# Output product of both token chunks in the front part, with one split of its weights, and the first layer norm statistics beside it

## The chip, the cores and the metric

The kernel runs on one core of a Trainium2 chip. A core has a matrix engine (TensorE, PE in the profile), a vector engine (VectorE, DVE), an activation engine (ScalarE, ACT), a general engine (GpSimd, POOL), a sync engine that issues most transfers (SyncE, SP), and 16 DMA engines. Each engine runs its own list of instructions in order; semaphores order them against each other. The metric is the device time of one execution, in microseconds (us).

## The reference, cut to what matters

One layer of a decoder trunk over 1024 prompt tokens and 8 x 8 sample tokens. Two token mixers (sparse attention and gated linear attention) run on the same input; what follows them is what the change touches:

```python
    branch_a = attn @ w_attn_o
    branch_b = o_b @ w_gla_o
    merged = jax.nn.sigmoid(z['gate_a']) * branch_a + jax.nn.sigmoid(z['gate_b']) * branch_b
    return merged @ w_out, k_a, v_a, k_i, s_new.astype(x.dtype)

def residual_block(x, mix_out, ln1_g, ln1_b, w_ff1, w_ff2, ln2_g, ln2_b):
    h = layer_norm(DN_ALPHA * x + mix_out, ln1_g, ln1_b)
    ff = jnp.square(jax.nn.relu(h @ w_ff1)) @ w_ff2
    return layer_norm(DN_ALPHA * h + ff, ln2_g, ln2_b)
```

Widths: 1024 model features, 4096 FF features. `layer_norm` takes the mean and the mean square over the features of each token. DN_ALPHA is 2 ** 0.25.

## The kernel before, in words

**Tiles.** Features lie on the 128 partitions, tokens along the free axis. The 1088 tokens are three chunks, counted from zero here as in the code: chunk 0 (tokens 0 to 383), chunk 1 (384 to 767), chunk 2 (768 to 1087, the rest of the prompt and the samples). A 1024 x 1024 weight is eight columns `f` of eight 128 x 128 blocks `k`.

**Split products.** Every product of full precision is three matmuls of a reduced-precision type (`mm3`): a weight and an input are split into a high half (an ACT copy that rounds) and a low half (a DVE or POOL subtraction of the high half), and TensorE adds high x high, high x low and low x high. A 128-column of `w_out` for one chunk is thus 8 x 3 = 24 matmuls of 128 x 384. Each weight costs a load (SP), an ACT copy and a subtraction.

**Front and back.** `front` holds the projections, both mixers for the prompt, and at its end the jobs that mix the branches (`mix_job`) and the output product of chunk 0 (`project_job`, matmuls into `pwo`). `back` opens other pools over the same memory. Its `project` runs the output product of chunk 1 (`outputs`), loading and splitting `w_out` a second time, then `feed` runs the feed-forward network in blocks of four or eight FF1 columns and all eight FF2 columns, for chunks 0 and 1 together, with the samples' attention (`at_scores`, `at_values`) in between, and then for chunk 2.

**Layer norm** (`ln`). The residual sum `z` is 8 tiles of 128 x 384 (`zx` for chunk 0, `z` for chunk 1); POOL adds them to one tile (`ls`, or the third part of `zx`) as they come. One matmul of ones gives the mean (`plm`); DVE subtracts it, ACT squares (`lq`), DVE and POOL add up the squares (`ls2`, `ls3`); one set of matmuls gives the mean square (`plv`); ACT takes the root and DVE the reciprocal (`lr`); TensorE spreads it (`plr`); DVE scales each `z`, ACT adds the bias and rounds to the high half of `h`, DVE makes the low half.

**FF stage.** `ff1_first` runs the first four FF1 columns side by side, over `k` as the tiles of `h` appear. `ff1_out` squares the positive part: ACT, DVE, ACT (high half of `a`), DVE or POOL (low half). `ff2_pair` runs the first two FF2 columns side by side, over the first three FF1 outputs and then the fourth; `ff2_out` adds to `acc`, the first time with two DVE operations that also add ALPHA times the two halves of `h`.

**What sets the order.** The code of each job is a generator that says what it needs next. `Order.run` steps the first generator whose needs are due, by a model of each engine's clock (`Clock`), and the instructions stand on each engine in the order in which they are so emitted. `Clock.take` models which buffer of a pool comes free first. All engine calls go through one helper, so they all have the same line in the profile (L260); tiles tell them apart. In the names of tiles, `w`, `wh`, `wl` are the halves of split weights, `wr` raw weights, `mg` the split merged branches, `sum` the merged branch of chunk 1 before its split.

In the front, weights of a job are loaded and split ahead of it into pages (`page`, 34 pages in two groups), which are free again after the job.

## Time and profile before

| | us |
|---|---|
| median of 3 runs | 2049.19 |
| lowest and highest run | 2048.11 and 2050.15 |
| the profiled execution | 2050.56 |
| its span, first to last instruction | 2048.9 |

The span is one execution on the chip. The profile gives for each engine its busy time and, for an idle stretch, the instruction that ended it (the releaser). A stretch of the span can be asked for with the busy time of each engine and the clock that TensorE was granted, as a share of full speed; a timeline lists one engine's instructions, equal neighbours merged, with the time at which a group starts and how long it lasts. Matmuls overlap: one of 128 x 384 is listed with 0.33 us and starts 0.17 us after the one before.

The front ends at about 1066 us, with the last product of chunk 0. The product of chunk 1 follows until 1109, then FF1 (to 1132) and FF2 (to 1153) of chunk 0, then FF1 and FF2 of chunk 1.

### The profile page before, as it was taken

The page shows a single profiled execution, that of the slowest core. Times are in us where ns is not written, and L with a number is a line of the kernel's source. Part 1 is how long each engine was busy: PE and PEld are TensorE (multiplying, and loading weights), DVE is VectorE, ACT ScalarE, POOL GpSimd, SP SyncE. Part 2 cuts the span into 40 slices and gives each one's busy share as a digit, 9 for nine tenths or more (in the row PEclk, how much of TensorE's full clock was granted, in tenths as well). Part 3 has the DMA queues.
Part 4 walks back from the last instruction along what each step waited for, and adds up shares of the span by engine and source line. Part 5 has one row for each costly group of instructions (what it writes and reads, how often), then busy time and mean ns, then how long its engine had stood idle before and what let it go on. Part 6 is the DMA issues. An engine that isn't in the chain of part 4 may idle for free.

```text
span 2048.9 us, 34577 instructions
## 1 busy us (share of the span) xinstructions
PE 2017.5 (98%) x12439; PEld 1949.7 (95%) x12439; DVE 1250.1 (61%) x2624; ACT 1115.4 (54%) x2217; POOL 787.4 (38%) x585
## 2 busy tenths in 40 slices
PE   9999999999999999999999999999999999999998
PEld 8999999999999999999989999998999999999998
DVE  7897767785655856641458645566554544466635
ACT  6687788887778466640134334545443232445544
POOL 5144232233311131231243335555654343364455
PEclk9999999999999999999999999999999999999999
DMA  9465212212132242373753145655533443145542
GB/s 323 184 210 158 94 35 70 80 53 86 43 115 84 77 148 69 101 239 129 255 202 101 40 123 157 183 147 152 155 93 108 135 132 98 58 136 163 185 149 94
DMA packets 186892, 264.51 MB, mean 129 GB/s; under 512 B 22352, under 2 KB 121680, under 8 KB 186720
## 3 DMA queue, kind: packets, MB, share of 16 engines
q1 hardware_dynamic: 179168, 236.87, 36.6%
q0 software_dynamic: 7552, 25.43, 4.2%
q8 instruction: 98, 1.61, 0.3%
q14 instruction: 74, 0.61, 0.1%
HBM read 212.72 MB, written 49.51 MB: 128 GB/s over the span
## 4 chain that ended last, share of the span: by engine, by line
PE 52%; issue 3%; DVE 2%; POOL 1%; ACT 1%; DMA 1%; SPq 0%; ACTq 0%; POOLq 0%; DVEq 0%
PE pf L260 33%; PE pwo L260 4%; PE pmb L260 4%; PE gate L260 2%; PE pma L260 2%; PE psc L260 2%; PE pob L260 1%; PE pst L260 1%; POOL w L260 1%; DVE aqz L260 0%; DMA ckr<-kT 0%; PE pov L260 0%; SPq L260 0%; ACT pp L260 0%; PE ppt L260 0%
## 5 line engine op out<-in xcount | busy, mean ns | idle before, releaser
L260 PE MATMUL pf<-a,w 128*128 128x384 f32 (+1 forms) x2304 | 397.5, 329 | 2.2 <-POOL a L260 1.3
L260 PE MATMUL pf<-h,w 128*128 128x384 f32 (+1 forms) x2304 | 395.7, 329 | 3.0 <-POOL w L260 1.8
L260 PEld LDWEIGHTS pf<-h,w 128*128 128x128 f32 x2304 | 380.1, 189 | 5.7 <-POOL w L260 2.1
L260 PEld LDWEIGHTS pf<-a,w 128*128 128x128 f32 x2304 | 378.5, 188 | 6.7 <-POOL a L260 1.8
L260 POOL TENSOR_TENSOR wl<-wr,wh 128x1024 fp32r<-128x1024 f32 (+1 forms) x67 | 152.8, 2284 | 422.1 <-ACT wh L260 335.6
L260 POOL TENSOR_TENSOR w<-wr,w 128x512 fp32r<-128x512 f32 x142 | 202.1, 1431 | 128.9 <-ACT w L260 117.9
L260 ACT ACTIVATE w<-wr 128x512 fp32r<-128x512 f32 x272 | 156.6, 618 | 36.9 <-PE pf L260 25.4
L260 DVE TENSOR_TENSOR w<-wr,w 128x512 fp32r<-128x512 f32 x130 | 134.0, 1038 | 52.8 <-ACT w L260 51.4
L260 DVE TENSOR_TENSOR acc<-acc,pf 128x384 f32<-128x384 f32 (+1 forms) x136 | 72.9, 538 | 93.8 <-PE pf L260 92.3
L260 PE MATMUL gate<-xh,wh 128*128 128x384 f32 (+1 forms) x384 | 128.8, 335 | 0.0
L260 POOL TENSOR_TENSOR a<-fr,a 128x384 fp32r<-128x384 f32 (+1 forms) x54 | 52.7, 975 | 194.3 <-ACT a L260 190.1
L260 PE MATMUL gate<-xh,wl 128*128 128x384 f32 (+1 forms) x384 | 125.5, 327 | 0.0
L260 PE MATMUL gate<-xl,wh 128*128 128x384 f32 (+1 forms) x384 | 125.4, 326 | 0.0
L260 ACT ACTIVATE wh<-wr 128x1024 fp32r<-128x1024 f32 (+1 forms) x76 | 75.1, 997 | 84.4 <-PE pmb L260 66.3
L260 ACT ACTIVATE fr<-pf 128x384 f32<-128x384 f32 (+1 forms) x96 | 44.8, 467 | 115.0 <-PE pf L260 113.1
L260 DVE TENSOR_TENSOR fr<-fr,pf 128x384 f32<-128x384 f32 (+1 forms) x96 | 50.8, 529 | 92.0 <-ACT fr L260 91.1
L260 ACT ACTIVATE a<-fr 128x384 fp32r<-128x384 f32 (+1 forms) x96 | 48.7, 508 | 81.2 <-DVE fr L260 79.7
L260 DVE TENSOR_SCALAR_CACHE_REDUCE jk<-sc,ga_f 128x1024 int8<-128x1024 f32 (+2 forms) x96 | 88.3, 919 | 1.7
L260 ACT ACTIVATE jkb<-sc,gb_f 128x896 int8<-128x896 f32 (+2 forms) x96 | 86.1, 897 | 5.6 <-DVE gb_f L260 3.2
L260 PE MATMUL psv<-wh,xh 128*128 128x256 f32 x288 | 80.7, 284 | 0.0
L260 PE MATMUL psv<-wl,xh 128*128 128x256 f32 x288 | 80.3, 283 | 0.0
L260 DVE CUSTOM_DVE_ANT_0 pp<-psq,msk 128x512 f32<-128x512 f32 (+3 forms) x96 | 51.4, 554 | 46.2 <-PE psq L260 44.9
(516 smaller groups left out, 5148.6 us busy)
## 6 DMA issues: line engine op xcount, KB each, us to landing
wr<-wff SPq DMA_DIRECT2D x256, 256.0 KB
wr<-w SPq DMA_DIRECT2D x42, 512.0 KB
ckr<-kT SPq DMA_DIRECT2D x256, 64.0 KB
ga_s<-gate SPq DMA_DIRECT2D x16, 544.0 KB
ci_s<-cig SPq DMA_DIRECT2D x16, 512.0 KB
kir<-ci_s SPq DMA_DIRECT2D x16, 512.0 KB
wr<-wout SPq DMA_DIRECT2D x13, 512.0 KB
mgp<-ga_s SPq DMA_DIRECT2D x16, 384.0 KB
```

The source lines that it names most:

```text
L260: r = f(*a, **k)
```

## The change

The output product of chunk 1 moves from the back into the front, behind that of chunk 0, with the same split weights. `project_job` keeps the eight split columns of `w_out` (`kept`); after column 6 of chunk 0 comes column 0 of chunk 1 (LAGC is 6), after column 7 the other seven. The merged branches of chunk 1 are split in the first four jobs (`mh`). The mean, the squares and the spread of 1/sigma of chunk 0 (`ln_first`) run beside the products of chunk 1; `ln_rest` is the second half of the former `ln`. The last three evictions of chunk 1 (NOUT) are left to `project` in the back, between the splits of the first FF1 weights and the scaling of chunk 0. FF1 of chunk 0 starts with two columns side by side (NFIRST) and two single ones; the first FF2 group has three columns for chunks 0 and 1. ALPHA times `h` (with ALPHA times the bias, `ab`) is written to `acc` by ACT in `emit_h`, so that the first `ff2_out` is one DVE addition. Fewer of the first weights are loaded in one piece, and split weights go to other pools (`place`). The pages that the last jobs may take are chosen by other names (`last`).

```diff
     def last(name):
-        return name[:2] == "mg" and name[2:].isdigit() or name[:2] in ("wr", "wh", "wl") and int(name[2:].split("_")[0]) >= state["last"]
+        return name[:2] == "mh" or name[:2] in ("wh", "wl") and int(name[2:].split("_")[0]) >= state["last"]
...
-    project_at = state["last"] = len(jobs)
+    state["last"] = len(jobs) + 5
+    project_at = len(jobs)
+    env["outs"] = []
+    kept = {}
...
+    def ln_first():
+        z = [resid[0][f // 2][:, f % 2] for f in range(8)]
+        on = zt["on"]
+        yield [rsum[0]]
+        pm = bank("plm")[:, :384]
+        pe.matmul(pm, on, rsum[0], start=True, stop=True)
+        yield [pm]
+        s2, s3 = small("ls2", 384), small("ls3", 384)
+        q = None
+        for f in range(9):
+            if f < 8:
+                dve.tensor_tensor(z[f], z[f], pm, op=OP.subtract)
+            if q is not None:
+                e, x = (pool, s3) if f in (4, 6) else (dve, s2)
+                e.tensor_tensor(x, x, q, op=OP.add)
+            if f < 8:
+                q = small("lq", 384) if f > 1 else None
+                act.activation(q if f > 1 else s3 if f else s2, z[f], AF.Square)
+            yield ()
+        dve.tensor_tensor(s2, s2, s3, op=OP.add)
...
+    def project(f, c, w):
+        ps = bank("pwo", True)[:, :384]
+        for k in range(8):
+            if k >= 6:
+                yield [mg[c][k][1]]
+            (h, l), a, b = mg[c][k], w[0][k], w[1][k]
+            pe.matmul(ps, a, h, start=k == 0, stop=False)
+            pe.matmul(ps, a, l, start=False, stop=False)
+            pe.matmul(ps, b, h, start=False, stop=k == 7)
+            if k % 2:
+                yield ()
+
+        def out():
+            unpin(ps)
+            z = zt[f - f % 2, c]
+            dve.scalar_tensor_tensor(z[:, f % 2], z[:, f % 2], ALPHA, ps, op0=OP.mult, op1=OP.add)
+            if f == 1:
+                rsum[c] = zt[0, c][:, 2]
+                pool.tensor_tensor(rsum[c], z[:, 0], z[:, 1], op=OP.add)
+            elif f:
+                pool.tensor_tensor(rsum[c], rsum[c], z[:, f % 2], op=OP.add)
...
+        if c and f >= 8 - NOUT:
+            env["outs"].append(out)
+        else:
+            out()
+
+    def other(f):
+        if f % 2 == 0:
+            x_load(f + 2, 1)
+        yield from project(f, 1, kept.pop(f))
 
     def project_job(f):
         def run(w):
+            if f == LAGC - 1:
+                x_load(0, 1)
+            kept[f] = w
...
+            yield from project(f, 0, w)
+            for g in range(2 * f, 2 * f + 2 if f < 4 else 0):
+                x = sums[f][:, g % 2]
+                m = page(f"mh{g}", F32R, [P, 2, 384])
+                act.activation(m[:, 0], x, AF.Copy, scale=0.5)
+                dve.scalar_tensor_tensor(m[:, 1], x, 0.5, f32(m[:, 0]), op0=OP.mult, op1=OP.subtract)
+                mg[1].append((m[:, 0], m[:, 1]))
+            if f >= LAGC:
+                yield from other(f - LAGC)
+            if f == 7:
+                order.add(ln_first(), at=0)
+                for k in range(8 - LAGC, 8):
+                    yield from other(k)
...
-            if self is W and 3 <= i < 8:
-                r = wide(f"{self.name}r{i}", F32, [P, 8, P])
+            if self is W and 3 <= i < 6:
+                r = wide(f"{self.name}r{i}", F32, [P, 8, P])[:, :kt]
                 sp.dma_start(r, src)
...
+            if f % 2 == 0 and c < 2:
+                acc[f // 2, c] = page(f"acc{f}{c}", F32)
             act.activation(t[:, 0, :n], z, AF.Identity, bias=b)
...
+            if c < 2:
+                act.activation(acc[f // 2, c][:, f % 2, :n], z, AF.Identity, bias=ab[:, f:f + 1], scale=ALPHA)
...
-    for f in range(8):
-        W.add(A["wout"][f], 8)
-
     def project():
-        raw, zs = ([x[f][:, i] for f in range(4) for i in range(2)] for x in (env["sums"], env["resid"]))
-        for _ in range(7):
+        for _ in range(4):
             W.load()
-        W.ahead(0, 0, NRW)
-        ks = range(8)
-        st = {f: page(f"mg{f}") for f in (7, 0, 1, 2, 3, 4, 5, 6)}
-        for f in ks:
-            act.activation(st[f][:, 0], raw[f], AF.Copy, scale=0.5)
-        for f in ks:
-            dve.scalar_tensor_tensor(st[f][:, 1], raw[f], 0.5, f32(st[f][:, 0]), op0=OP.mult, op1=OP.subtract)
-            mg[f, 1] = (st[f][:, 0], st[f][:, 1])
-        norm(0, zs, env["resid"][0][:, 2], 0, emit_h(0), 1)
-        yield from outputs(1, lambda f: W.get(f, 2, NRW), page, ks)
+        outs = env["outs"]
+        for i in range(4):
+            W.ahead(i, 0, NRW)
+            if i % 2 and len(outs) > 1:
+                outs.pop(0)()
+        for i, _ in enumerate(ln_rest(0, [x[:, i] for x in env["resid"][0] for i in range(2)], env["ln0"], 0, emit_h(0), 1)):
+            if i == 8:
+                outs.pop(0)()
+        z1 = [x[:, i] for x in env["resid"][1] for i in range(2)]
+        norm(1, z1, env["rsum"][1], 0, emit_h(1), 1)
+        yield ()
...
-        if first:
+        if first and c == 2:
             h, l = hc[f, c]
             dve.scalar_tensor_tensor(o, f32(h), ALPHA, ps[:, :n], op0=OP.mult, op1=OP.add)
             dve.scalar_tensor_tensor(o, f32(l), ALPHA, o, op0=OP.mult, op1=OP.add)
...
-                        if f < np_ == 4:
+                        if f < np_ == 4 and (c or f < NFIRST):
                             w4 = [w] if f == 0 else w4 + [w]
-                            if f == 3:
-                                yield from ff1_first(w4, c, a)
+                            if f == (3 if c else NFIRST - 1):
+                                yield from ff1_first(w4, c, a, None)
...
-                        elif f == np_:
-                            w0 = w
-                        elif f == np_ + 1:
-                            yield from ff2_pair((w0, w), c, a, np_)
+                        elif f < np_ + 1 + (c < 2):
+                            w3 = [w] if f == np_ else w3 + [w]
+                        elif f == np_ + 1 + (c < 2):
+                            yield from ff2_pair(w3 + [w], c, a, np_)
```

Up to the seventh product of chunk 0 the engines' instructions stand as before, but for the splits `mh`. Three places show what moves. In the rows, names carry the number of their buffer; `wh70` and `wl70` are the eighth column of `w_out` in the front, and a row's brackets name the engines or queues that it waits for.

First, DVE at the end of chunk 0's product. Before:

```order
L260 SCALAR_TENSOR_TENSOR zx4_11596<-zx4_11596,pwo_11698 128x384 [waits PE_49]
L260 TENSOR_TENSOR wl70_0_11726<-wr70_0_11659,wh70_0_11725 128x1024 [waits DMAHW0_49,Activation_49,Pool_49]
L260 SCALAR_TENSOR_TENSOR zx6_11664<-zx6_11664,pwo_11729 128x384 [waits DMAHW1_49,PE_49]
L260 SCALAR_TENSOR_TENSOR zx6_11664<-zx6_11664,pwo_11756 128x384 [waits PE_49]
L260 TENSOR_TENSOR w0_0_11831<-wr0_0_11811,w0_0_11831 128x512 [waits DMAHW2_49,Activation_49]
L260 TENSOR_TENSOR w0_1_11834<-wr0_4_11813,w0_1_11834 128x512 [waits DMAHW3_49,Activation_49]
L260 SCALAR_TENSOR_TENSOR mg0_11838<-sum0_11220,mg0_11838 128x384 [waits Activation_49]
```

The same place now:

```order
L263 SCALAR_TENSOR_TENSOR zx40_11612<-zx40_11612,pwo_11727 128x384 [waits PE_49]
L263 TENSOR_TENSOR wl70_0_11756<-wr70_0_11687,wh70_0_11755 128x1024 [waits DMAHW0_49,PE_49,Activation_49]
L263 SCALAR_TENSOR_TENSOR zx60_11692<-zx60_11692,pwo_11758 128x384 [waits DMAHW1_49]
L263 SCALAR_TENSOR_TENSOR zx01_11725<-zx01_11725,pwo_11788 128x384 [waits DMAHW2_49,DVE_49]
L263 SCALAR_TENSOR_TENSOR zx60_11692<-zx60_11692,pwo_11814 128x384 [waits PE_49]
L263 SCALAR_TENSOR_TENSOR zx01_11725<-zx01_11725,pwo_11841 128x384 [waits PE_49]
L263 TENSOR_TENSOR zx00_11485<-zx00_11485,plm_11877 128x384 [waits PE_49]
```

The split of the eighth column waits for TensorE where it did not; the matmul that it waits for is the last of `pwo_11788`, the first column of chunk 1. The second weight split and the splits of the merged branch are gone from here, and the mean of chunk 0 is subtracted behind the second eviction of chunk 1.

Second, DVE at the seam, from the reciprocal of chunk 0 on. Before (chunk 1's evictions `z41`, `z61` and weights of `w_out`, w8 the first of FF1):

```order
L260 SCALAR_TENSOR_TENSOR z41_11952<-z41_11952,pwo_12093 128x384 [waits PE_49]
L260 TENSOR_TENSOR w8_0_12126<-wr8_0_12003,w8_0_12126 128x512 [waits DMAHW0_49,Activation_49]
L260 RECIPROCAL lr_12116<-lr_12116 128x3
L260 SCALAR_TENSOR_TENSOR zx0_11483<-zx0_11483,lnp_100,plr_12156 128x384 [waits PE_49]
L260 SCALAR_TENSOR_TENSOR zx0_11483<-zx0_11483,lnp_100,plr_12156 128x384
L260 SCALAR_TENSOR_TENSOR zx2_11529<-zx2_11529,lnp_100,plr_12156 128x384
L260 SCALAR_TENSOR_TENSOR h00_12161<-zx0_11483,lnp_100,h00_12161 128x384 [waits Activation_49]
```

Now (w0 to w3 are the first four FF1 columns, `zx41` and `zx61` the residuals of chunk 1):

```order
L263 SCALAR_TENSOR_TENSOR zx41_11868<-zx41_11868,pwo_11959 128x384 [waits DMAHW4_49,PE_49]
L263 RECIPROCAL lr_11982<-lr_11982 128x3 [waits Activation_49]
L263 TENSOR_TENSOR w0_0_12115<-wr0_0_12101,w0_0_12115 128x512 [waits DMAHW6_49,Activation_49]
L263 TENSOR_TENSOR w0_1_12118<-wr0_4_12103,w0_1_12118 128x512 [waits DMAHW7_49,Activation_49]
L263 TENSOR_TENSOR w1_1_12124<-wr1_4_12107,w1_1_12124 128x512 [waits DMAHW1_49,Activation_49]
L263 SCALAR_TENSOR_TENSOR zx41_11868<-zx41_11868,pwo_11992 128x384 [waits PE_49]
L263 TENSOR_TENSOR w2_0_12133<-wr2_0_12109,w2_0_12133 128x512 [waits DMAHW2_49,Activation_49]
L263 TENSOR_TENSOR w2_1_12136<-wr2_4_12111,w2_1_12136 128x512 [waits DMAHW3_49,Activation_49]
L263 TENSOR_TENSOR w3_1_12146<-wr3_12113,w3_1_12146 128x512 [waits DMAHW4_49,Activation_49]
L263 SCALAR_TENSOR_TENSOR zx61_11957<-zx61_11957,pwo_12022 128x384 [waits DMAHW5_49,PE_49]
L263 SCALAR_TENSOR_TENSOR zx00_11485<-zx00_11485,lnp_100,plr_12006 128x384 x2
```

Six halves of weights and two evictions stand between the reciprocal and the first scaling, where none stood. On TensorE the spread (`plr`) now stands in the sixth column of chunk 1's product, with 60 matmuls of the product behind it, and the mean of chunk 1 between the sixth and the seventh block of FF1's first two columns. POOL makes the other two halves of these weights and the sums of chunk 1's residuals.

Third, SP behind the last weight of the front. Before:

```order
L260 DMA wr70_0_11659<-wout 128x1024 [waits DMAHW0_49,PE_49,Pool_49]
L260 DMA zx6_11664<-xT 128x2x384 [waits DMAHW1_49]
L260 DMA wr0_0_11811<-wout 128x512 [waits DMAHW2_49]
L260 DMA wr0_4_11813<-wout 128x512 [waits DMAHW3_49]
L260 DMA wr1_0_11815<-wout 128x512 [waits DMAHW4_49]
L260 DMA wr1_4_11817<-wout 128x512 [waits DMAHW5_49]
```

Now:

```order
L263 DMA zx61_11957<-xT 128x2x384 [waits DMAHW5_49,DVE_49]
L263 DMA wr0_0_12101<-wff1 128x512 [waits DMAHW6_49]
L263 DMA wr0_4_12103<-wff1 128x512 [waits DMAHW7_49]
L263 DMA wr1_0_12105<-wff1 128x512 [waits DMAHW0_49]
L263 DMA wr1_4_12107<-wff1 128x512 [waits DMAHW1_49]
L263 DMA wr2_0_12109<-wff1 128x512 [waits DMAHW2_49]
L263 DMA wr2_4_12111<-wff1 128x512 [waits DMAHW3_49]
L263 DMA wr3_12113<-wff1 128x1024 [waits DMAHW4_49,PE_49,Pool_49]
```

The second load of `w_out` is gone, and the first FF1 columns are loaded in its place; the fourth of them waits for TensorE, for the last matmul of chunk 1's fourth column.

More of the change, by code (lines that the diff above doesn't have):

```diff
@@ L46 @@
 NRW = 6
+NFIRST = 2
+NOUT = 3
+LAGC = 6
 NBW = 5
@@ L391, in front @@
     order = Order(clock)
+    eps = env["eps"]
+    pool.memset(eps, 1e-5)
     PGS = (("pz", NPZ), ("pg", NPG - NPZ))
@@ L1785, in front @@
     gp = {}
-    sums = env["sums"] = []
+    sums = []
     def gp_load(i):
@@ new lines, in front, with x_load @@
+    kept = {}
+    def x_load(f, c):
+        if f < 8:
+            zt[f, c] = env["xpage"](f"zx{f}{c}", F32, (P, 3, 384))
+            sp.dma_start(zt[f, c][:, :2], A["xT"][f:f + 2, :, 384 * c:384 * c + 384].rearrange("f p t -> p f t"))
+    def ln_first():
[18 more added lines that the diff above has]
+        dve.tensor_tensor(s2, s2, s3, op=OP.add)
+        yield [s2]
+        pv = bank("plv")
+        for j in range(3):
+            pe.matmul(pv[:, j:j + 1], s2[:, j * P:j * P + P], on[:, :1], start=True, stop=True)
+        yield [pv[:, :3]]
+        r3 = tiny("lr")
+        act.activation(r3[:, :3], pv[:, :3], AF.Sqrt, bias=eps)
+        yield [r3[:, :3]]
+        dve.reciprocal(r3[:, :3], r3[:, :3])
+        yield [r3[:, :3]]
+        r = env["ln0"] = bank("plr", True)
+        for j in range(3):
+            pe.matmul(r[:, j * P:j * P + P], r3[:, j:j + 1].to_broadcast([P, P]), idf, start=True, stop=True)
@@ L1846, in run @@
-            ps = bank("pwo", True)[:, :384]
-            yield from mm3(ps, w[0], w[1], [x[0] for x in mg], [x[1] for x in mg])
-            unpin(ps)
-            z = zt[f - f % 2]
-            dve.scalar_tensor_tensor(z[:, f % 2], z[:, f % 2], ALPHA, ps, op0=OP.mult, op1=OP.add)
-            rsum = zt[0][:, 2]
-            if f == 1:
-                pool.tensor_tensor(rsum, z[:, 0], z[:, 1], op=OP.add)
-            elif f:
-                pool.tensor_tensor(rsum, rsum, z[:, f % 2], op=OP.add)
@@ L1909, in front @@
     order.run(list(order.streams))
+    while order.streams:
+        order.run(list(order.streams))
 def back(ph, tc, env, A, O):
@@ L1940, in sub @@
             dve.tensor_sub(out, a, b)
-    for name, shape, dt, bufs in (("pg", [P, 2, 384], F32, NBP), ("cw", [P, 2, 512], F32, NCW), ("sm", [P, 384], F32, NBS), ("on", [P, P], F32, 1),
+    for name, shape, dt, bufs in (("pg", [P, 2, 384], F32, NBP), ("cw", [P, 2, 512], F32, NCW), ("sm", [P, 384], F32, NBS), ("on", [P, P], F32, 1), ("ab", [P, 8], F32, 1),
                                   ("tall", [P, 4, TS], F32, 1), ("rcs", [64, 8], F32, 1), ("r3", [P, 8], F32, 2), ("msk", [P, 1024], BF, 3),
@@ L2006, in place @@
     def place(i):
-        if 12 <= i < 20:
-            return xpage
-        return wide if (i < 12 or i >= last_at) and i % 4 >= 2 else w_tile
+        if 4 <= i < 12:
+            return xpage if i < 8 else wide
+        return wide if (i < 4 or i >= last_at) and i % 4 >= 2 else w_tile
     flags = set()
@@ L2026, in back @@
     mg, hc, acc = {}, {}, {}
+    ab = own("ab", [P, 8])
+    pool.tensor_scalar(ab, lnp[:, 1, :], ALPHA, None, op0=OP.mult)
     normed = set()
@@ L2065, in ln, with ln_rest @@
             pe.matmul(r[:, o:o + P], r3[:, j:j + 1].to_broadcast([P, P]), idf, start=True, stop=True)
+        yield from ln_rest(c, z, r, gi, emit, tag)
+    def ln_rest(c, z, r, gi, emit, tag):
+        n = CH[c][1]
         yield [r[:, :n]]
@@ L2480, in merge, with ff1_first @@
         yield from outputs(2, lambda f: V.get(8 + f, 1, 2), wide)
-    def ff1_first(ws, c, a):
+    def ff1_first(ws, c, a, more=None):
         n = CH[c][1]
@@ L2487, in ff1_first @@
         for ks in [[k] for k in range(KFIRST)] + [list(range(KFIRST, 8))]:
+            if more and ks[-1] == 7:
+                more()
             for f, w in enumerate(ws):
@@ L2540, in ff2_out @@
         n = CH[c][1]
-        if first and f % 2 == 0:
+        if first and f % 2 == 0 and c == 2:
             acc[f // 2, c] = page(f"acc{f}{c}", F32)
         o = acc[f // 2, c][:, f % 2, :n]
-        if first:
+        if first and c == 2:
             h, l = hc[f, c]
@@ L2579, in feed @@
                         if c == cc[0]:
-                            ws[f] = W.get(i0 + f, 2 if c == 2 else min(2, np_ + 7 - f), NRW)
+                            ws[f] = W.get(i0 + f, 2 if c == 2 else 3 - f if f < 4 else min(2, np_ + 7 - f), NRW)
                         if c == 1 and f in (np_ + 3, np_ + 6):
```

30 lines of the change are left out of this document (16 added, 14 removed).

## The prediction

> **What bounds the kernel now.** I read the page first, for the engine that sets the time.
>
> ```profile
> span 2048.9 us, 34577 instructions
> PE 2017.5 (98%) x12439; PEld 1949.7 (95%) x12439; DVE 1250.1 (61%) x2624; ACT 1115.4 (54%) x2217; POOL 787.4 (38%) x585
> ```
>
> TensorE is busy 98% of the span, so an edit is worth what it takes from TensorE's own stretches, not what it saves on VectorE (DVE) or the DMA queues. Next I asked for the stages around the change, cut at the matmuls where one kind of work ends: six clean output products, the eight products of chunk 1, chunk 0's first FF1, its FF2, chunk 1's FF1. Columns: stretch, its length, busy of PE, PEld, DVE, ACT, POOL, granted clock, DMA share, GB/s.
>
> ```profile
> 1040.96:1065.91 24.95, 24.95 (x145) 24.80 (x144) 9.00 (x11) 5.60 (x7) 10.41 (x6) 1.00 0.62 221
> 1065.91:1109.46 43.55, 39.58 (x208) 37.63 (x207) 34.61 (x51) 20.27 (x40) 18.52 (x16) 0.92 0.27 88
> 1109.46:1132.12 22.66, 19.66 (x100) 18.44 (x99) 19.16 (x30) 11.26 (x22) 9.27 (x7) 0.92 0.30 93
> 1132.12:1152.79 20.67, 19.38 (x109) 17.87 (x109) 18.02 (x29) 8.44 (x18) 8.26 (x6) 1.00 0.25 78
> 1152.79:1169.62 16.83, 16.83 (x98) 16.83 (x97) 6.75 (x13) 3.43 (x7) 1.01 (x1) 1.00 0.01 1
> ...
> 1073.86:1080.68 6.82, 5.87 (x17) 5.51 (x18) 4.10 (x7) 0.00 (x0) 0.47 (x1) 0.50 0.22 60
> ```
>
> The first row prices a product: 24.95 / 6 = 4.16 us, or 0.173 us a matmul (24 each). The last stage prices 96 back-part matmuls at 16.83. The three between do more than their matmuls need. The short row is why a wait costs more than its idle time: after the holes of 1071 to 1075 the clock stood at 0.50 for 6.82 us, 3.4 us lost. TensorE's timeline shows the holes and the matmuls of layer norm (`plm` the mean, `plv` the squares, `plr` the spread of 1/sigma); the bracket is the idle time before and who ended it.
>
> ```profile
> 1067.33 3.43 PE L260 MATMUL pwo<-mg,w 128*128 128x384 f32 x18 [0.72 <-DVE w L260]
> 1071.72 0.45 PE L260 MATMUL pwo<-mg,w 128*128 128x384 f32 x1 [0.96 <-DVE mg L260]
> 1073.27 0.44 PE L260 MATMUL pwo<-mg,w 128*128 128x384 f32 x1 [1.10 <-DVE mg L260]
> 1074.81 6.75 PE L260 MATMUL pwo<-mg,w 128*128 128x384 f32 x21 [1.10 <-DVE mg L260]
> 1081.39 0.81 PE L260 MATMUL plm<-zx,on 128*128 128x384 f32 x2
> 1081.74 17.12 PE L260 MATMUL pwo<-mg,w 128*128 128x384 f32 x96
> 1098.70 0.72 PE L260 MATMUL plv<-on,ls 128*128 128x1 f32 x6
> 1099.29 4.43 PE L260 MATMUL pwo<-mg,w 128*128 128x384 f32 x24
> 1103.56 0.83 PE L260 MATMUL plr<-idf,lr 128*128 128x128 f32 x6
> 1104.15 5.47 PE L260 MATMUL pwo<-mg,w 128*128 128x384 f32 x30
> ...
> 1115.07 6.07 PE L260 MATMUL pf<-h,w 128*128 128x384 f32 x25 [1.75 <-POOL w L260]
> 1120.98 0.81 PE L260 MATMUL plm<-ls,on 128*128 128x384 f32 x2
> ```
>
> ```profile
> 1134.06 0.44 PE L260 MATMUL pf<-a,w 128*128 128x384 f32 x1 [0.41 <-ACT a L260]
> 1135.14 4.27 PE L260 MATMUL pf<-a,w 128*128 128x384 f32 x23 [0.63 <-POOL a L260]
> 1139.60 0.83 PE L260 MATMUL plv<-on,ls 128*128 128x1 f32 x6 [0.19 <-DVE ls L260]
> ...
> 1171.56 0.44 PE L260 MATMUL pf<-a,w 128*128 128x384 f32 x1 [0.41 <-ACT a L260]
> ```
>
> Every releaser at the seam is a split: of the gated sums (`mg`), of a weight (`w`) or of an FF1 output (`a`). That work is what the change moves ahead or spreads.
>
> **What goes.** plm costs 0.35 us to the next start, plus 0.3 that the 96 products behind it take beyond 96 x 0.173; plv and plr 0.59 each. So the eight products need 8 x 4.16 + 0.67 + 2 x 0.59 = 35.1 us and took 43.55: 8.4 over. Chunk 0's FF1 needs 16.83 + 0.67 = 17.5 and took 22.66: 5.2 over. Its FF2 needs 16.83 + 1.18 = 18.0 and took 20.67: 2.7 over. Together **16.3 us** of waits and half clock, the most that this seam can give. The hole at 1171.56, chunk 1's FF2 behind four FF1 outputs that end together, stays: the group of three still asks for the third output after six matmuls.
>
> **What comes.** The products, the layer-norm matmuls and FF1/FF2 are the same in number, so TensorE's own work is unchanged; eight weight loads and their splits go, on engines that aren't the bound (nothing by itself, hidden before by the products themselves). The ACT copies `acc` replace two DVE operations per output; ACT is busy 3.43 of 16.83 us in the clean stage, room enough. I walked the new order engine by engine with these durations:
>
> ```profile
> 1058.27 1.22 DVE L260 TENSOR_TENSOR wl<-wr,wh 128x1024 fp32r<-128x1024 f32 x1
> 1101.11 0.68 DVE L260 TENSOR_TENSOR w<-wr,w 128x512 fp32r<-128x512 f32 x1
> 1101.71 0.17 DVE L260 RECIPROCAL lr<-lr 128x3 f32<-128x3 f32 x1
> 1104.43 1.66 DVE L260 SCALAR_TENSOR_TENSOR zx<-zx,lnp,plr 128x384 f32<-128x384 f32 x3 [2.55 <-PE plr L260]
> 1119.81 1.66 DVE L260 SCALAR_TENSOR_TENSOR h<-zx,lnp,h 128x384 fp32r<-128x384 f32 x3
> 1066.12 0.56 DVE L260 SCALAR_TENSOR_TENSOR zx<-zx,pwo 128x384 f32<-128x384 f32 x1 [3.61 <-PE pwo L260]
> ```
>
> ```profile
> 1062.64 1.01 POOL L260 TENSOR_TENSOR zx<-zx,zx 128x384 f32<-128x384 f32 x1 [2.29 <-issue]
> 1102.63 1.28 POOL L260 TENSOR_TENSOR w<-wr,w 128x512 fp32r<-128x512 f32 x1
> ```
>
> ```profile
> 1099.62 1.14 ACT L260 ACTIVATE w<-wr 128x512 fp32r<-128x512 f32 x2
> ```
>
> *The last weight.* All eight pairs are now kept, and pages run out: the low half of the eighth, `wl70`, waits for the end of the first chunk-1 product, whose weight page it takes, and the third matmul of the next product waits for `wl70`. Two matmuls run under it. From the last matmul's start: 0.34 to its end, 1.22 split, about 0.1 hand-overs, less 3 x 0.173: **1.2 us**. Behind it in DVE stand chunk 0's seventh eviction and its POOL sum; plm stands 30 matmuls (5.2 us) after the eighth product and needs 0.56 + 1.01, so nothing follows.
>
> *Statistics of chunk 0.* plm to plv now spans 18 + 24 + 18 = 60 matmuls, 10.4 us. DVE needs 13 operations of about 0.55, 7.2 us, with ACT squares between: about 8, inside. plv to plr, 18 matmuls or 3.1 us, holds a root, an eviction (0.56) and a reciprocal: inside. A miss would put its excess straight on TensorE.
>
> *The seam.* The reciprocal ends 0.16 + 0.56 + 0.17 + hand-overs, 0.9 us, behind the fifth chunk-1 product; plr stands 12 matmuls, 2.1 us, behind it. So from the reciprocal to the end of the front TensorE has 1.2 + 0.6 (plr) + 60 x 0.173 = 12.2 us. DVE has six splits, two evictions, three scalings and the first low half of h: 6 x 0.68 + 2 x 0.56 + 4 x 0.53 = 7.3 us. The second weight's copies on ACT wait for plr (they take a buffer that its input leaves), so DVE, done with the first weight after 2 x 0.68, idles 1.2 + 0.8 + 1.14 - 1.36 = 1.8: 9.1 in all, if nothing blocks it. But POOL's operations can:
>
> ```profile
> 1034.64 2.75 DVE L260 TENSOR_TENSOR sum<-mgp 128x384 f32<-128x384 f32 x1
> ...
> 1034.58 5.08 POOL L260 TENSOR_TENSOR wl<-wr,wh 128x1024 fp32r<-128x1024 f32 x2 [3.06 <-ACT wh L260]
> ```
>
> A DVE sum of two SBUF tiles that takes 0.55 elsewhere took 2.75 here, started 0.06 us behind a POOL split. Two POOL splits (1.28) and three sums (1.01) lie in the seam: up to 5.6 us more, 14.7 against 12.2. Not all of them meet a two-input operation (evictions and scalings read PSUM and one SBUF tile), so I take the first h as just in time: no wait, with 2.5 as the other end. Then DVE makes one h in 2 x 0.53 = 1.06 us and TensorE eats one in 6 x 0.173 = 1.04: level. Chunk 1's plm stands behind six of them, 6.2 us, and needs five more h, the last eviction and a POOL sum: 5 x 1.06 + 0.56 + 1.0 to 1.5 (when it meets a DVE operation) = 6.9 to 7.4. It waits **0.9 us**, between nothing and 1.2.
>
> The Trainium skill, "SBUF — State Buffer", section "Who interferes with whom", says that a DVE instruction with two SBUF inputs and a POOL instruction that reads SBUF exclude each other, the first to issue holding the port pair to its end. The 2.75 us row agrees. By that rule the seam's splits are paid twice where they meet, which speaks against putting them there.
>
> *The rest.* Chunk 0's third and fourth FF1 outputs now end 24 matmuls apart, and FF2 asks for the fourth after 27, 4.7 us, against a chain of three operations of about 0.55 (ACT, DVE, ACT) and a POOL one of 1.0. Chunk 1's statistics get 114 matmuls from plm to plv, 20.0 us at 16.83 / 96; before they had 1139.60 - 1120.98 = 18.6 and missed by 0.19. In my walk the weights `w6` and `w11` come some 0.2 us ahead of need. For these I take **0.5 us**, between 0 and 3.
>
> **Sum:** 16.3 - 1.2 - 0.9 - 0.5 = 13.7 us. The profiled execution took 2050.56 us (span 2048.9 and 1.66 around it), 1.4 above the median of 2049.19; against it the sum gives 2036.9, against the median, which I forecast, **2035.5**.
>
> **Rivals.** (1) *The waits all hide*: wl70 beside a stretched product, plm just in time. Then 2049.2 - 16.3 = 2032.9. The order speaks against it: wl70's wait is hard. (2) *The wait moves to the seam on DVE*: each of the five POOL operations blocks DVE once, h comes 2.5 us late, and a window of half clock follows:
>
> ```profile
> 1114.90:1118.30 3.40, 3.23 (x10) 3.23 (x11) 3.40 (x5) 0.49 (x1) 1.80 (x2) 0.51 0.77 228
> ```
>
> Price: 2.5 and 3.40 x 0.49 = 1.7 of clock: 2039.7; with the rest at its bound (3 for 0.5) 2042.2. For it: DVE's 14.7 against 12.2. Against it: the evictions and scalings, 0.53 to 0.56 in all rows above, give POOL room. (3) *The half clock follows wl70 alone.* Half clock here came behind one hole of 2.48 us:
>
> ```profile
> 1428.57 0.54 PE L260 MATMUL psc<-ckh,aqz 128*128 128x512 f32 x1 [2.48 <-DVE aqz L260]
> 1428.85:1432.30 3.45, 3.45 (x10) 2.33 (x9) 3.31 (x8) 0.63 (x1) 0.74 (x1) 0.51 0.58 176
> ```
>
> A hole of 1.2 is under that, and the two of 1134 (0.41 and 0.63) left the stage at 1.00; if it falls all the same: 2035.5 + 1.7 = 2037.2. The Trainium skill, "TensorE: Matmul & The Clock Gate", "What's actually happening", lets the clock fall after an idle window of about 3.4 us; here less than that was enough, and the rows decide.
>
> (4) *It doesn't do what it says*: the seam's time is not waits but slow matmuls, and the products cost in the front what they cost in the back: no change, 2049. Against it: front products run at 0.173 us, and the brackets name waits. (5) *Slower*: FF1's first weights come late. In the back their loads come out of SP's queue at the pace at which buffers fall free:
>
> ```profile
> 1079.84 37.76 SPq L260 DMA_DIRECT2D wr<-wff  x14
> ```
>
> 2.7 us each. If the seven loads of the first four weights stood behind the last product (pages that overlay those it reads, in SP's one queue), TensorE would wait 7 x 2.7 = 18.9, a split of 1.3 and two windows of half clock, 3.4: 23.6 us in place of 0.9, so 2035.5 + 22.7 = 2058.2. It turns slower than before by 0.2% once the wait with its clock passes 0.9 + 13.7 + 4.1 = 18.7 us. Against it: in the new order the first six loads wait only for earlier transfers, and the fourth weight for a product 14 us ahead of the end.
>
> **How the numbers follow.** About 0.2% (4.1 us) is what a measurement of this kernel can tell from no change. Chances: the forecast with its bounds (2033.5 to 2039) 0.60; (1) 0.12; (2), or chunk 1's statistics late by as much, 0.15; (3) 0.05; (4) 0.04; (5) 0.04. The bottom is (1) less the 1.1 us by which the fastest run lay under the median: 2031.8. The top is (2) with its bound, 2042.2; outside stand (4), (5) and little else. Faster by over 0.2%: 0.92; within: 0.04; slower: 0.04.
>
> **What would show it.** Right: the idle before `pwo` is one hole of about 1 us behind `wl`; none behind `mg`; plv and plr of chunk 0 without a bracket; the first `pf<-h,w` within 0.3 us of the last `pwo`; a bracket of about 0.6 us before chunk 1's plm, ended by POOL; clock 1.00 throughout; the two holes of `a` once, in chunk 1. Wrong: `pf<-h,w` waiting for DVE h by over 2 us, plv waiting for DVE `ls`, a clock of 0.5 in the seam, or any new hole in the sample's attention behind it (`psc`, `pst`), whose order moves a little.

## The result, and the profile after

| | before | after |
|---|---|---|
| median, us | 2049.23 | 2037.48 |
| lowest and highest run, us | 2048.11 and 2050.15 | 2035.11 and 2039.56 |
| the profiled execution, us | 2050.56 | 2039.02 |

The ratio is 0.9943 with a 95% interval of 0.9925 to 0.9960: faster by 0.4 to 0.75%. Here and below a median or ratio leaves slow runs out; there was one, of 3081.14 us at a granted clock of 0.60, in e1. The page of after, first its busy times:

```profile
span 2037.3 us, 34522 instructions
PE 2012.7 (99%) x12439; PEld 1949.4 (96%) x12439; DVE 1227.1 (60%) x2597; ACT 1114.6 (55%) x2217; POOL 775.4 (38%) x582
```

TensorE's count is the same 12439, and its idle time fell from 31.4 us to 24.6. The stretches that answer to the stages of before: from the hole behind the eighth weight to the end of the front (products), FF1 of chunk 0, FF2 of chunk 0, FF1 of chunk 1. Columns as before.

```profile
1067.02:1101.83 34.81, 34.81 (x204) 34.55 (x204) 21.40 (x35) 12.17 (x23) 14.46 (x14) 1.00 0.24 77
1101.83:1119.29 17.46, 17.46 (x99) 17.10 (x99) 13.37 (x25) 12.50 (x26) 5.77 (x5) 1.00 0.00 0
1119.29:1138.27 18.98, 18.55 (x109) 17.95 (x109) 16.24 (x28) 11.00 (x22) 8.63 (x7) 1.00 0.24 80
1138.27:1155.07 16.80, 16.80 (x97) 16.80 (x97) 4.78 (x10) 4.52 (x10) 1.01 (x1) 1.00 0.02 6
```

The clock is 1.00 in all four, and TensorE is busy through products and FF1 without a gap. FF1 takes 17.46 us where it took 22.66. TensorE's timeline of after, the matmuls that had brackets before and those that have one now:

```profile
1066.75 0.44 PE L263 MATMUL pwo<-mg,wl 128*128 128x384 f32 x1 [1.02 <-DVE wl L263]
1075.89 0.81 PE L263 MATMUL plm<-zx,lon 128*128 128x384 f32 x2
1086.93 0.72 PE L263 MATMUL plv<-lon,ls 128*128 128x1 f32 x6
1090.73 0.83 PE L263 MATMUL plr<-idf,lr 128*128 128x128 f32 x6
1101.83 6.52 PE L263 MATMUL pf<-h,w 128*128 128x384 f32 x36
1108.19 0.85 PE L263 MATMUL plm<-zx,on 128*128 128x384 f32 x2
1128.91 0.72 PE L263 MATMUL plv<-on,ls 128*128 128x1 f32 x6
1136.42 2.01 PE L263 MATMUL pf<-a,w 128*128 128x384 f32 x10 [0.43 <-POOL w L263]
1157.02 0.44 PE L263 MATMUL pf<-a,w 128*128 128x384 f32 x1 [0.40 <-ACT a L263]
1158.10 12.23 PE L263 MATMUL pf<-a,w 128*128 128x384 f32 x69 [0.64 <-POOL a L263]
...
1414.34 0.47 PE L263 MATMUL psc<-ckh,aqz 128*128 128x512 f32 x1 [2.45 <-DVE aqz L263]
1416.67 0.36 PE L263 MATMUL pso<-idf,sa 64*128 64x64 f32 x1 [0.62 <-DVE sa L263]
```

At the seam one hole is left ahead of a product, the one of the eighth weight; the statistics and the first FF1 have no bracket. The two of `a` stand once, in chunk 1. The last two rows lie behind the seam, in the samples' attention; the first of them was there before (2.48), the second was not; e9 below shows that this second one is not the change's doing.

Where the time went, by matmuls that both traces have: chunk 1's first `pf<-a` with a bracket came at 1171.56 and comes at 1157.02, 14.54 us earlier. 0.45 of that was there at a matmul of the front ahead of the change (916.31 and 915.86), so the seam gives **14.1 us**. The hole of 2.45 begins 14.2 us earlier than before (1428.57 - 2.48 against 1414.34 - 2.45), and the span ends 11.6 us earlier: behind that hole 2.6 us are given back. The same 10 us of the two traces, from just ahead of the end of that hole, before (first) and after:

```profile
1428.30:1438.30 10.00, 9.73 (x42) 8.00 (x43) 8.41 (x23) 2.74 (x5) 4.93 (x5) 0.83 0.48 139
```

```profile
1414.10:1424.10 10.00, 9.14 (x32) 7.21 (x33) 7.33 (x22) 1.74 (x4) 3.19 (x3) 0.66 0.47 139
```

A clock of 0.83 over 10 us is 3.4 us of half clock, 0.66 is 6.8: a second stretch of half clock followed the same hole, 1.7 us, and 0.62 is the new hole; together 2.3 of the 2.6.

### The profile page after: what moved, and what is told of

Same layout as the page of the kernel before. It is cut to its first block, busy times and chain, and to the rows that moved or that the text cites. A ratio compares the mean times of both kernels' runs of the same rounds, so it can differ in the third digit from the quotient of the medians.

```text
span 2037.3 us, 34522 instructions
## 1 busy us (share of the span) xinstructions
PE 2012.7 (99%) x12439; PEld 1949.4 (96%) x12439; DVE 1227.1 (60%) x2597; ACT 1114.6 (55%) x2217; POOL 775.4 (38%) x582
## 4 chain that ended last, share of the span: by engine, by line
PE 53%; issue 2%; ACT 1%; DVE 1%; POOL 1%; SPq 0%; DMA 0%; ACTq 0%; POOLq 0%; DVEq 0%
PE pf L263 34%; PE pwo L263 5%; PE pmb L263 4%; PE gate L263 2%; PE pma L263 2%; PE psc L263 2%; PE pob L263 1%; PE pst L263 1%; SPq L263 0%; PE pov L263 0%; ACT pp L263 0%; PE ppt L263 0%; POOL w L263 0%; POOL wl L263 0%; ACT as L263 0%
## 5 line engine op out<-in xcount | busy, mean ns | idle before, releaser
L263 POOL TENSOR_TENSOR w<-wr,w 128x512 fp32r<-128x512 f32 x135 | 191.1, 1423 | 124.9 <-ACT w L263 114.5
L263 ACT ACTIVATE w<-wr 128x512 fp32r<-128x512 f32 x256 | 147.6, 618 | 39.0 <-PE pf L263 25.9
L263 DVE TENSOR_TENSOR w<-wr,w 128x512 fp32r<-128x512 f32 x121 | 126.8, 1053 | 55.8 <-ACT w L263 54.4
L263 DVE TENSOR_TENSOR acc<-acc,pf 128x384 f32<-128x384 f32 (+1 forms) x152 | 81.4, 539 | 104.9 <-PE pf L263 104.7
```

The lines of the kernel that those rows point to most:

```text
L263: r = f(*a, **k)
```

## The experiments

Three questions: which parts of the change carry the gain, whether the holes that are left have the causes that the order gave them, and what takes back 2.6 us behind the seam. The ratios are to the kernel before on the same chip; the changed kernel itself, run again (e9), had 0.9938 (0.9925 to 0.9952). Where medians are set against 2037.48, they come from other chips, on which the kernel before had 2050.23 to 2050.44 in place of 2049.23.

**Two splits of the weights (e1).** The products stay in the front, now all behind chunk 0's, but eight further jobs load and split the columns again.

```diff
             if f >= LAGC:
-                yield from other(f - LAGC)
+                pass
             if f == 7:
                 order.add(ln_first(), at=0)
-                for k in range(8 - LAGC, 8):
-                    yield from other(k)
+        return run
+
+    def other_job(f):
+        def run(w):
+            kept[f] = w
+            yield from other(f)
         return run
...
+    for f in range(8):
+        job((A["wout"][f], 8, P), other_job(f))
```

> The changed kernel, but the eight columns of the output weight are loaded and split a second time for chunk 1's products, which still run in the front, all behind chunk 0's. Theory A (the gain is the place: the sums split ahead and the statistics beside the products; the spared splits were hidden work): eight more loads and splits of 1.22 us on VectorE, 9.8 us, lie beside 33 us of products and cost nothing, and the eighth column of chunk 0 no longer waits for a page, so the hole of 1.02 us goes: about 2036.5 us, no hole from 1040 to 1135. Theory B (the spared splits are the gain): up to 9.8 us come back, 2043 to 2047, as holes before pwo that end with a weight split.

Measured: 2040.54 us, ratio 0.9953 (0.9937 to 0.9969). The hole of 1.02 is gone; a new one stands beside chunk 0's statistics, on TensorE and on DVE:

```profile
1077.78 0.45 PE L263 MATMUL pwo<-mh,wl 128*128 128x384 f32 x1 [2.71 <-DVE wl L263]
```

```profile
1075.15 0.98 DVE L263 TENSOR_TENSOR ls<-ls,lq 128x384 f32<-128x384 f32 x1 [0.17 <-ACT lq L263]
1076.05 0.54 DVE L263 SCALAR_TENSOR_TENSOR zx<-zx,pwo 128x384 f32<-128x384 f32 x1
1076.51 3.16 DVE L263 TENSOR_TENSOR wl<-wr,wh 128x1024 fp32r<-128x1024 f32 x2
```

The weight's split stands in DVE's list behind the squares of chunk 0 and comes 2.7 us late, with a stretch of half clock behind. Neither theory held in full: most of the gain comes with two splits as well, so it is the place with its order. The spared splits look worth 2 to 3 us (by the ratios 0.9953 against 0.9943 and 0.9938, by the medians 3.1), but these intervals overlap, so the size isn't resolved; the trace shows where it would come from, since the second splits share DVE with the statistics.

**Statistics behind the front (e5).** `ln_first` goes; the back runs the whole chain once the front is done.

```diff
-                order.add(ln_first(), at=0)
...
+        norm(0, [x[:, i] for x in env["resid"][0] for i in range(2)], env["rsum"][0], 0, emit_h(0), 1)
```

> The changed kernel, with chunk 0's statistics not beside chunk 1's products but behind the front, as one chain (mean, squares, root, spread). Theory A (the products of chunk 1 are the cover of this chain): TensorE stands idle from the last pwo to the first h: last evictions and sum 2, mean 0.8, squares 8, plv, root and spread 2.5, first h 2 us: about 14 to 16 us less what the last products cover, with a window of half clock (1.7) behind; 2037.5 + 14 to 18 = 2051 to 2055 us, slower than before the change. Theory B (what pays is the split of the sums and weights alone): the hole is hidden by other work and the time stays within 2 us of 2037.5.

Measured: 2055.87 us, ratio 1.0029 (1.0018 to 1.0040), slower than before the change. TensorE's timeline:

```profile
1102.06 0.91 PE L263 MATMUL plm<-zx,on 128*128 128x384 f32 x2 [1.14 <-POOL zx L263]
1108.28 1.44 PE L263 MATMUL plv<-on,ls 128*128 128x1 f32 x6 [5.31 <-DVE ls L263]
1113.88 1.65 PE L263 MATMUL plr<-idf,lr 128*128 128x128 f32 x6 [4.17 <-DVE lr L263]
1117.49 0.69 PE L263 MATMUL pf<-h,w 128*128 128x384 f32 x1 [1.96 <-ACT h L263]
```

The chain stands bare: 12.6 us of holes at these four steps, and from 1104.7 to 1121.75 the clock stood at 0.51, with TensorE busy for 7.10 of it, which is 3.5 us more; the rest of the 18.4 isn't traced. Theory A holds, 0.9 us above its range. Moving the products without the statistics loses time here: the products are the chain's cover.

**FF1 with four columns (e6)**, `NFIRST = 4`.

> The changed kernel with NFIRST 4: chunk 0's first FF1 takes four columns side by side, as before the change. Theory A: two columns are what lets FF1 start, and with four the holes behind the third and fourth weight come back (0.92 + 0.33 + 1.75 us and 1.7 of half clock before the change), and the two before pf<-a of chunk 0 (0.41 + 0.63): 2037.5 + 5.7 = about 2043. Theory B: all four weights are split 3.5 us ahead of the first pf in the changed kernel's trace, so only the two holes before pf<-a come back: about 2038.5.

Measured: 2044.90 us, ratio 0.9974 (0.9965 to 0.9984). The time is near A's, the holes are neither theory's. TensorE, ACT and POOL:

```profile
1123.87 0.61 PE L263 MATMUL pf<-a,w 128*128 128x384 f32 x2 [3.83 <-ACT w L263]
1125.23 1.65 PE L263 MATMUL pf<-a,w 128*128 128x384 f32 x4 [0.74 <-POOL w L263]
```

```profile
1122.78 0.52 ACT L263 ACTIVATE a<-fr 128x384 fp32r<-128x384 f32 x1 [0.62 <-DVE fr L263]
1123.21 2.70 ACT L263 ACTIVATE w<-wr 128x512 fp32r<-128x512 f32 x5
```

FF1 itself runs without a hole, as B said: its weights are there. What is late are the first weights of FF2: their copies stand in ACT's list behind all four FF1 outputs. With two columns and two single ones, `W.ahead` puts them between the columns: in the changed kernel ACT begins one at 1114.54 and one at 1118.21, between FF1 outputs. That is what NFIRST buys, not an earlier start of FF1.

**Last evictions in the front (e10)**, `NOUT = 1`.

> The changed kernel with NOUT 1: of chunk 1's last three evictions two stay in the front, only the last is left to the back. Theory A: their place decides nothing but chunk 1's mean, which has 0.1 us to spare: 2037.5 within 1 us. Theory B: in the front they stand ahead of the first FF1 weights' splits on VectorE and hold them up until their products end: first h or first weight late, a bracket before pf<-h of 1 to 3 us, perhaps with half clock: 2038.5 to 2042.

Measured: 2043.88 us, ratio 0.9970 (0.9959 to 0.9981). TensorE's first FF1 matmul and DVE ahead of it:

```profile
1106.27 0.44 PE L263 MATMUL pf<-h,w 128*128 128x384 f32 x1 [3.71 <-ACT h L263]
```

```profile
1094.27 0.55 DVE L263 SCALAR_TENSOR_TENSOR zx<-zx,pwo 128x384 f32<-128x384 f32 x1 [4.22 <-PE pwo L263]
1098.43 0.55 DVE L263 SCALAR_TENSOR_TENSOR zx<-zx,pwo 128x384 f32<-128x384 f32 x1 [3.61 <-PE pwo L263]
1098.90 6.08 DVE L263 TENSOR_TENSOR w<-wr,w 128x512 fp32r<-128x512 f32 x5
```

Theory B, larger than it said. DVE waits 4.22 and 3.61 us for products whose evictions stand first, with five splits queued behind; then the splits and the first h come in one run, the first h 3.71 us late, and half clock follows.

**FF2 as before (e11)**: two columns side by side, `acc` by two operations of DVE.

> The changed kernel with chunk 0's and chunk 1's first FF2 as before the change: two columns side by side in place of three, and acc written by two operations of VectorE (16 more of about 0.55 us over the two chunks, 8.8 us) in place of one and a copy by ScalarE. Theory A: beside chunk 0's FF2 VectorE is busy 16.2 of 19.0 us, 4.4 more don't fit: chunk 1's squares or h are late, a bracket before plv, plr or pf<-h of 1 to 3 us: 2038.5 to 2041. Theory B: only waits off the path grow: 2037.5 within 1 us.

Measured: 2040.19 us, ratio 0.9954 (0.9940 to 0.9967). Theory A: chunk 1's squares are late, and half clock follows. The edit undoes two parts at once, so it doesn't tell which of them did it.

```profile
1132.54 0.83 PE L263 MATMUL plv<-on,ls 128*128 128x1 f32 x6 [1.36 <-DVE ls L263]
```

**The page of the eighth weight (e2, e7).** e2 sets `LAGC = 5`. e7 keeps six, but runs chunk 1's first column behind column 5 of chunk 0 and none between 6 and the end of 7:

```diff
-            if f == LAGC - 1:
+            if f == LAGC - 2:
                 x_load(0, 1)
...
-            if f >= LAGC:
-                yield from other(f - LAGC)
+            if f == LAGC - 1:
+                yield from other(0)
             if f == 7:
                 order.add(ln_first(), at=0)
-                for k in range(8 - LAGC, 8):
+                for k in range(1, 8):
```

> The changed kernel with LAGC 5: chunk 1's first column stands one product of chunk 0 earlier, so the page that the eighth column's low half takes is free 8.3 us ahead of need in place of 0. Theory: the hole of 1.02 us before pwo goes and nothing takes its place: 1.0 us less than the changed kernel, about 2036.5 us. Rival: the split moves to GpSimd (2.45 us) or chunk 0's statistics, whose last product now stands later, fall behind: a new bracket of 1 us or more before plm, plv or pwo, and 2037.5 us or more.

> The changed kernel, with chunk 1's first column already behind column 5 of chunk 0, and columns 6 and 7 of chunk 0 next to each other, so that the last weight's page is free 4.2 us ahead of need and chunk 0's statistics start 12 matmuls earlier against chunk 1's products. Theory: the hole of 1.02 us before pwo goes and, other than with LAGC 5, the first pf does not wait for h, since 75 matmuls in place of 60 stand behind the spread of 1/sigma: 1.0 us less than the changed kernel, about 2036.5. Rival: the split of the last weight, now 2.45 us on GpSimd, or the later first sum is late: 2037.5 or more, with a bracket before pwo, plm or pf.

Measured: e2 2041.93 us, ratio 0.9957 (0.9943 to 0.9971); e7 2036.52 us, ratio 0.9932 (0.9916 to 0.9949). The hole of 1.02 is gone from both traces, so its cause was the page. In e2 the rival came true in its time, though the bracket stands at `pf` and not at the matmuls that it named:

```profile
1104.36 0.44 PE L263 MATMUL pf<-h,w 128*128 128x384 f32 x1 [2.25 <-ACT h L263]
1105.23 8.49 PE L263 MATMUL pf<-h,w 128*128 128x384 f32 x38 [0.43 <-DVE h L263]
```

One product fewer stands behind the last one of chunk 0, so its statistics have 4.16 us less cover. Of that, 2.7 us are missing at its end (from the reciprocal to the end of the products are 9.8 us in place of 12.5), and the first h is late. e7 frees the page without taking that cover, and has neither hole; its 1.0 us, too, is seen in the trace and not resolved in the medians.

**Two columns for chunk 1 too (e3)**, `f < NFIRST` for both chunks.

> The changed kernel, with chunk 1's first FF1 as two columns side by side and two single ones, as chunk 0's is. Theory: the two holes before pf<-a of chunk 1's FF2 (0.40 and 0.64 us) are there because four FF1 outputs end together; with the last two 24 matmuls apart they go: 1.0 us less than the changed kernel, about 2036.5 us. Rival: two columns side by side use up one h in 1.04 us, faster than VectorE makes them beside the additions to acc (1.5 us each), and FF1 waits for h: a bracket of 1 us or more before pf<-h, 2037.5 us or more.

Measured: 2036.82 us, ratio 0.9938 (0.9921 to 0.9954). The brackets of 0.40 and 0.64 are gone and no other has come behind the edit at the seam (one of 0.62, at 1037.92, stands in the front, ahead of all that the edit touches). The 1.0 us is seen in the trace; in the medians, against 2037.48 and 2036.90 for the changed kernel, it isn't resolved.

**The hole of 2.45 us (e4, e8).** In the trace of after, DVE, then POOL, at that place:

```profile
1407.81 6.66 DVE L263 CAST aqz<-aq 64x32 fp32r<-64x32 f32 x8
```

```profile
1406.63 4.89 POOL L263 TENSOR_TENSOR ckl<-ckr,ckh 128x1024 fp32r<-128x1024 f32 x2
```

Eight casts of 0.17 us each took 6.66. Beside the two key splits on POOL and the two splits of 128x512 that follow them, four of the casts took 1.25, 2.39, 1.21 and 1.21 us. e4 moves the casts to ACT; e8 leaves them and takes the keys' splits from POOL.

```diff
-                        dve.tensor_copy(x, f32(aq[r:r + 64, 4 * g + par:4 * g + par + 3:2]).rearrange("p h (b q) -> p b h q", b=2))
+                        act.activation(x, f32(aq[r:r + 64, 4 * g + par:4 * g + par + 3:2]).rearrange("p h (b q) -> p b h q", b=2), AF.Copy)
```

```diff
-        sub(*(x.rearrange("p a b -> p (a b)") for x in (l, r, f32(h))))
+        dve.tensor_sub(*(x.rearrange("p a b -> p (a b)") for x in (l, r, f32(h))))
```

> The changed kernel, with the eight small casts of the samples' queries (64x32) on ScalarE in place of VectorE. Theory A: the 2.45 us hole before psc is a cast of 0.17 us that VectorE could not run for 2.39 us beside a GpSimd split of 128x1024; on ScalarE it isn't held up: the hole, the one of 0.62 us behind it and the two windows of half clock go, 2.45 + 0.62 + 3.4 = 6.5 us of the profiled execution's 2039.0, so about 2032.5; no clock under 1.00 but at the ends. Theory B: the data of the casts come late: ScalarE waits as long, and the hole stays at about 2.4 us.

> The changed kernel, with all low halves of the samples' keys (ckl) on VectorE; eight of 32 were on GpSimd. Theory A (VectorE's small operations with inputs from SBUF are held up by a GpSimd operation that runs beside them, here 2.4 us for a key of 128x1024): the hole of 2.45 us before psc and the 0.62 behind it go or shrink to 1.3 (the GpSimd splits of 128x512 that are left), and no half clock follows: 2.5 to 6.5 us less than the changed kernel's profiled 2039.0, 2032.5 to 2036.5. Theory B: VectorE, with eight more splits of 1.22 us, is late instead: a hole of the same size behind ckl, 2037 or more.

Measured: e4 2038.82 us, ratio 0.9946 (0.9930 to 0.9963); e8 2033.03 us, ratio 0.9917 (0.9901 to 0.9934). In e4 the hole is gone, but another of its kind stands 85 us earlier, with half clock behind it; TensorE, DVE, POOL:

```profile
1329.03 0.24 PE L263 MATMUL pso<-idf,sa 64*128 64x64 f32 x1 [2.38 <-DVE sa L263]
```

```profile
1326.62 2.25 DVE L263 TENSOR_SCALAR sa<-sa,rcs 64x128 f32<-64x128 f32 x1
```

```profile
1326.41 2.39 POOL L263 TENSOR_TENSOR ckl<-ckr,ckh 128x1024 fp32r<-128x1024 f32 x1
```

So theory A's cause is right and its sum was wrong: the next small DVE operation met the next POOL split, and a `pf<-a` at 1409 waited 0.89 and 0.63 us for its split inputs, in the order that moved. In e8 both holes before `psc` and the one before the last `plr` are gone. The groups of the casts (count: shortest, median and longest in ns), after and e8:

```profile
L263 DVE CAST aqz<-aq x32: 170/176/2393, 1185.5 to 1414.3; 64x32 fp32r<-64x32 f32 x32
```

```profile
L263 DVE CAST aqz<-aq x32: 165/174/1258, 1186.3 to 1413.8; 64x32 fp32r<-64x32 f32 x32
```

The longest falls to the length of a POOL split of 128x512 (1.26 to 1.29), the longest kind that is left beside them. The Trainium skill, "SBUF — State Buffer", section "Who interferes with whom", lists casts and `tensor_scalar` among the DVE operations that can take the port pair shared with GpSimd; these rows agree.

**The changed kernel again (e9).**

> The changed kernel itself, beside the next three on one chip. Expected 2037.5 us. Its trace should show the holes of the first one at the same matmuls (1.02 before pwo, 0.43, 0.40 and 0.64 before pf<-a, 0.97 and 2.45 before psc). If the windows of half clock behind the 2.45 us hole are drawn by where the hole falls against a grid of 3.41 us and not by its length, their number (two in the first trace) need not be the same, and single runs lie up to 3.4 us apart.

Measured: 2036.90 us, ratio 0.9938 (0.9925 to 0.9952); the holes that were named are there again, and the 2.45 us hole was followed by one stretch of half clock, where the first trace had two. The hole of 0.62 behind it is not there: in the same kernel `pso` comes without a bracket. In e3, whose trace has the hole of 2.45 too, it is there. TensorE in e9 (two rows) and e3:

```profile
1414.14 0.77 PE L263 MATMUL psc<-ckh,aqz 128*128 128x512 f32 x1 [2.45 <-DVE aqz L263]
1416.97 0.37 PE L263 MATMUL pso<-idf,sa 64*128 64x64 f32 x1
...
1416.39 0.27 PE L263 MATMUL pso<-idf,sa 64*128 64x64 f32 x1 [0.68 <-DVE sa L263]
```

The 10 us behind the hole, in e9 and in e3:

```profile
1413.90:1423.90 10.00, 9.76 (x43) 8.04 (x44) 7.35 (x23) 2.66 (x5) 5.10 (x5) 0.83 0.46 137
```

```profile
1413.80:1423.80 10.00, 9.07 (x48) 7.77 (x49) 8.42 (x24) 2.90 (x5) 5.65 (x5) 1.00 0.46 139
```

Eleven of the fourteen traces have the hole of 2.45 to 2.48. In three of them (after, e1, e3) the clock is still 1.00 in the first microsecond behind it; these three, and no others, have a bracket of 0.62 to 0.68 before `pso`. In the other eight the clock of that microsecond is 0.50 to 0.87, TensorE is slower on its way to `pso`, and DVE's `sa` is there in time.

**Three edits together (e12)**: those of e3, e7 and e8.

> The changed kernel with three edits that each took holes away alone: chunk 1's first column behind column 5 of chunk 0, chunk 1's first FF1 as two columns and two single ones, the low halves of the samples' keys on VectorE. If the holes are independent, their gains add: 1.0 + 1.0 + 4.5 = 6.5 us of 2037.5: 2031.0, and no hole from 1040 us to the end but the 0.43 before pf<-a. If they hide one another or the seam's order tips, 2032 to 2034 with a new bracket.

Measured: 2031.30 us, ratio 0.9906 (0.9891 to 0.9921), 5.6 us under the changed kernel on the same chip, and faster than each edit alone. The time is within 0.3 us of the one expected if the gains add; the trace isn't quite, since two holes of 0.64 have come that were not expected. Holes that are left at and behind the seam:

```profile
1135.69 2.01 PE L263 MATMUL pf<-a,w 128*128 128x384 f32 x10 [0.42 <-POOL w L263]
1403.44 0.62 PE L263 MATMUL pf<-a,w 128*128 128x384 f32 x2 [0.64 <-POOL a L263]
1496.14 0.61 PE L263 MATMUL pf<-a,w 128*128 128x384 f32 x2 [0.64 <-POOL a L263]
```

## Why the prediction was right, step by step

The forecast was 2035.5, the median is 2037.48, inside the range and 2.0 over the forecast.

- *16.3 us of waits and half clock at the seam, nothing of it work.* Right: products and FF1 now take what their matmuls need (17.46 us for FF1, against 17.5 worked out), at a clock of 1.00. Rival (4) falls. e5, e6, e10 and e11 put time back at one place each, 18.4, 7.4, 6.4 and 2.7 us by their medians against 2037.48; together 35 us, three times the gain, so the parts hold each other up and don't add.
- *The last weight, 1.2.* Right: the bracket before `pwo` at 1066.75 is 1.02, and from start to start the matmul comes 1.37 us behind its neighbour in place of 0.17, so 1.2. No half clock followed, here or in the eight other traces with this hole; rival (3) falls. e2 and e7 show that the page was the cause.
- *Statistics of chunk 0, nothing.* Right; e2 shows what a product less of cover costs.
- *The seam on DVE.* The reciprocal began at 1089.32 and the first h was done at 1100.93, 11.6 us, inside the 9.1 to 14.7; I took "just in time" of 12.2, and it was 0.9 early. POOL's blocking is there: the rows below, DVE at the seam, have two splits in 2.08 us where 1.36 was enough, one in 1.38 for 0.68, three in 3.81 for 2.04, 3.2 us in all; POOL has its sums and splits beside each of them. Rival (2) was 0.9 us away; e2 and e10 show its outcome, a late first h and a stretch of half clock, though by other causes (less cover, evictions ahead of splits).

```profile
1089.40 2.08 DVE L263 TENSOR_TENSOR w<-wr,w 128x512 fp32r<-128x512 f32 x2
1092.79 1.38 DVE L263 TENSOR_TENSOR w<-wr,w 128x512 fp32r<-128x512 f32 x1 [1.30 <-ACT w L263]
1094.56 3.81 DVE L263 TENSOR_TENSOR w<-wr,w 128x512 fp32r<-128x512 f32 x3
1100.33 0.60 DVE L263 SCALAR_TENSOR_TENSOR h<-zx,lnp,h 128x384 fp32r<-128x384 f32 x1
```

- *Chunk 1's plm, 0.9.* Mis-sized: it measured nothing. Its chain was reckoned from an h that comes just in time; with h 0.9 us earlier POOL's sum ended at 1108.07 (the row below), 0.1 us ahead of plm at 1108.19.

```profile
1106.81 1.26 POOL L263 TENSOR_TENSOR zx<-zx,zx 128x384 f32<-128x384 f32 x1 [6.84 <-DVE zx L263]
```

- *The rest, 0.5.* It was 1.0: FF2 of chunk 0 took 18.98 against 18.0 worked out. About 0.6 of it is the hole behind a weight, as my walk feared (a bracket of 0.43, and the overlap with the matmul before it is lost too); the rest isn't traced to one place. The holes of chunk 1's `a` stayed, as forecast; e3 shows why.
- *Sum at the seam, 13.7.* 16.3 - 1.2 - 0 - 1.0 = 14.1 measured. That it is so near is in part luck: 0.9 too much for plm and 0.5 too little for the rest go against each other.
- *Nothing changes behind the seam* (the sum has no term for it). This held, as far as the traces show, although the first trace has what the prediction gave as a mark of error, a new hole in the samples' attention. By e9 that hole and the second stretch of half clock are draws of one execution: the same kernel has neither, and its profiled execution took 2036.90, where the sum, taken from the profiled 2050.56, gave 2036.9. To meet it so closely is luck, as the two terms above show.
- *The 2.0 us between forecast and median.* The forecast set the 13.7 against a median, as if executions drew the same half clock before and after. The four runs of after fall into two pairs: 2035.11 and 2035.94 us at mean clocks of 0.997 and 0.998, 2039.02 and 2039.56 at 0.996 and 0.996; the median is the middle between the pairs. A stretch of half clock costs 1.7 us and takes 0.0008 from the mean clock (half of 3.4 us, of 2037), so two stretches fit the 3.1 to 4.5 us between the pairs. Where in the kernel the clock fell is known only for profiled runs, so how much of the 2.0 us is this draw stays open.
